# Latent attention: the doubled keys' scores of two maximum tiles formed together on both 64-row tiles of the array

## The chip, the cores and the metric

The kernel runs on one core of one Trainium2 chip. A core has a matrix engine (TensorE, PE in the profile, its weight loads PEld), VectorE (DVE), ScalarE (ACT), GpSimd (POOL) and SyncE (SP, which here only starts DMAs). Matmuls write to PSUM, which the program holds as one tile `PB` of eight banks of 512 columns. The metric is device time in microseconds, the median of several runs; lower is better. Beside the runs there is one profiled execution, from which all views below are taken.

## What is computed

Two layers of a backbone: windowed attention, then latent attention; the change is in the second layer. Cut to what matters:

```python
def attend(qn, qr, kn, kr, v):                 # 16 heads, 1024 queries, 256 + 1024 = 1280 keys
    s = (jnp.einsum("bqhd,bkhd->bhqk", qn, kn)     # 64 dimensions, keys of the head
         + jnp.einsum("bqhd,bkd->bhqk", qr, kr)) * scale   # 32 dimensions, keys shared by the heads
    p = jax.nn.softmax(s, axis=-1)
    return jnp.einsum("bhqk,bkhd->bqhd", p, v)
```

The softmax needs, for each query, a number to subtract before the exponential. The kernel takes the maximum over all 1280 keys of scores that are formed once in a cheap way (one matmul pass over the high parts), and then forms the scores proper, with the shift already added by one more row of the product.

## The kernel before

**Units.** The work of the layer's attention is cut into 32 units (class `UnitB`): a unit is one head and one half of the queries (512). Unit number `ui` belongs to head `ui // 2`; `e` is the head's place in its pair, `half` the half of the queries. The order of PE, ACT and DVE is the order of the code (a manual schedule), POOL and SP follow the recorded order too. What decides when something runs is therefore the place in the loop over `units` and the semaphores between engines.

**The array in two row tiles.** The keys have 64 rows (64 dimensions), so two products of 64 rows run side by side on the upper and the lower half of the array: `t` = 0 and 1. The 1280 keys lie in `kt` and `kr1` as 768 columns on each half: columns 0 to 511 hold keys 0 to 511 on rows 0 to 63 and keys 512 to 1023 on rows 64 to 127; columns 512 to 767, the last 256 keys, stand on both halves. These are the doubled keys.

**Maximum tiles** (`top(b)`, b = 0 to 3, 128 queries each). Four matmuls of 512 columns (L1260, two passes on two row tiles) fill two banks; then the doubled keys' part, two matmuls of 256 columns (L1263), both on the row tile `b % 2`, fill half of a third bank. VectorE reduces the 1280 columns to a negated maximum (L1265). All four tiles use the same three banks `psm`, so each tile's first matmul waits for the reduction before it.

**Shift** (`shift`): PE transposes the four columns of maxima into `pm_bank` (L1269), VectorE spreads them (L1270), ScalarE copies (L1275).

**Scores** (`score(i, a, b)`, i = 0 to 4, 256 keys each): five passes on two row tiles, ten matmuls of 512 columns (L1291; the fifth pass, of 36 rows, adds the shift), into one of two pairs of banks (`slot()` alternates). `expo(i)` on ScalarE takes the exponential of the 1024 columns (L1297), after which GpSimd adds up the sums (L1301, L1305). A slot is free for the next score when its exponential is done.

**Values and the finish.** `PV` multiplies the exponentials by the values (20 matmuls, L1313) into `pv_bank`; `fin` copies half of it (L1328, ACT), `fin1` adds the other half (L1332, DVE); `fin2` transposes the sums (L1342), VectorE reduces them (L1343) and, for every second head, takes the reciprocal (L1346); `fin3` (L1357, L1358, L1360) scales the output.

**The order in one round of the loop** (unit `u`; `pu`, `ppu` are the units before it, `nu`, `nnu` after it): u.score(0) with nu.top(2) inside it after two of its five passes; u.score(1) with nu.top(3) inside it after four; products that make keys for the next pair in two rounds of four (`make_K`, L126 to L128); pu.PV; nu.shift; fin3 of ppu and fin2 of pu; nnu.top(0); pu.fin1; u.score(2), u.score(3), nnu.top(1), u.score(4). The rounds with `ui % 8 == 0` also make values (`make_V`), with fin1 ahead of that. So a round, from one PV to the next, holds 25 score pairs (a pair is the same pass on both row tiles), eight pairs of L1260 and eight single L1263.

Of the kernel before, what the change touches and what calls it, by code (L numbers as in the profile page):

```python
# [13 lines left out]
ALU = mybir.AluOpType  # L14
AX = mybir.AxisListType
# [6 lines left out]
TOK = SEQ + CTX  # L22
# [38 lines left out]
def kernel(ctx: ExitStack, tc: tile.TileContext, t, out, dbg=None):  # L61
    nc = tc.nc
# [4 lines left out]
    PB = ppool.tile([128, 8, 512], F32, name="PB")  # L67
# [56 lines left out]
    def mm3(o, a, b, first, last):  # L124
        (ah, al), (bh, bl) = a, b
        nc.tensor.matmul(o, ah, bh, start=first, stop=False)  # L126
        nc.tensor.matmul(o, al, bh, start=False, stop=False)  # L127
        nc.tensor.matmul(o, ah, bl, start=False, stop=last)  # L128
# [177 lines left out]
    class Pieces:  # L306
# [6 lines left out]
        def load(self, n=1):  # L313
            for _ in range(n):
                if self.todo:
                    bi, k = self.todo.pop(0)
                    c0 = blocks[bi]
                    st = shp(stg.next(), 2, 256)
                    src = w_in[k * 128 : (k + 2) * 128, c0 : c0 + 256]
                    load(out=st, in_=src.rearrange("(k p) n -> p k n", p=128))  # L320
                    self.held.append((bi, k, st))
# [119 lines left out]
    def proj_t(bi, gp, c):  # L441

        W = wt[bi]
        ps = pss()
        if gp:
            o = shp(ps, 2, 256)
            m = [hw[gp][:, :, s] for s in range(2)]
        else:
            o = ps[:, 0:258]
            m = [hT[0][:, s] for s in range(2)]  # L450
        cs = slice(c * 128, c * 128 + 128)
        for k in range(8):
            b = [x[:, :, k, :] if gp else x[:, k, :] for x in m]
            mm3(o, [W[:, s, k, cs] for s in range(2)], b, k == 0, k == 7)
        if gp == 0:
            bias[bi, c] = biases()
            nc.vector.tensor_copy(bias[bi, c], ps[:, 256:258])
        return ps
# [330 lines left out]
    for i, (gp, c) in enumerate([(1, 0), (1, 1), (2, 0), (2, 1)]):  # L789
        held.append((1, gp, c, proj_t(1, gp, c)))  # L790
        if i == 0:
            ps = pst()
# [16 lines left out]
    for c in range(2):  # L809
        ps = proj_t(1, 0, c)  # L810
# [6 lines left out]
    for bi in range(2, 8):  # L817
        for i, (gp, c) in enumerate([(0, 0), (0, 1), (1, 0), (1, 1), (2, 0), (2, 1)]):
            ps = proj_t(bi, gp, c)
# [7 lines left out]
    for bi in (8, 9):  # L827
        for c in range(2):
            ps = proj_t(bi, 0, c)
# [38 lines left out]
    for ui, u in enumerate(units):  # L868
# [11 lines left out]
        for ci in range(u.m):  # L880
# [10 lines left out]
            i = u.g * u.m + ci - 1  # L891
# [182 lines left out]
    def g_tile(bi, p, half=None, bank=None):  # L1074
        c0 = blocks1[bi][1]
        W = wt1[bi]
        if half != 1:
            gps[bi] = pss() if bank is None else bank
        ps = gps[bi]
        for j in (0, 1) if half is None else (half,):  # L1080
            for k in range(8):
                mm3(
                    ps[:, j * 256 : j * 256 + 256],
                    [W[:, s, k, j * 128 : j * 128 + 128] for s in range(2)],
                    [hT1[p][:, s, k, :] for s in range(2)],
                    k == 0, k == 7,
                )
        if half == 0:
            return
        gg = ev.next()  # L1090
        nc.scalar.activation(gg, ps, AF.Silu)
        ch = (c0 - 800) // 128
        load(out=g1_d[ch : ch + 2, :, (p - 1) * 256 : p * 256].rearrange("c p n -> p c n"), in_=shp(gg, 2, 256))

    nx = norm_x(src1(4), xr, junk)
    for ti in range(NT):
        n = ti + 3
# [45 lines left out]
    kr1, kr2 = r_at(12, 768), (r_at(112, 512), r_at(15, 256))  # L1143
# [6 lines left out]
    otr = Ring(F, [0, 4], 1024)  # L1150
    rbr = Ring(F, [8, 9], 256)
    mxr = Ring(F, [44, 44.5], 128)
    psm = PB[:, 0:3, :]
    pm_bank = PB[:, 2, 256:384]
    slots = [PB[:, 3:5, :], PB[:, 5:7, :]]
    pv_bank = PB[:, 7, :]

    def slot():
        slots.reverse()
# [22 lines left out]
                nc.gpsimd.tensor_copy(kr[p : p + 4], const[p : p + 4, 0:1].to_broadcast([4, n]))  # L1182

    def make_V(quad, x, x0=psm[:, 0:2]):
        for t0, ps in ((0, x0), (4, PB[:, 7:8]), (2, x)):
            nt = min(2, NP - t0)
            for j in range(2 * nt):
                ti = 2 * t0 + j
                o = ps[:, j // 2, (j % 2) * 256 : (j % 2) * 256 + 256]
                for k in range(2):  # L1190
                    mm3(
                        o,
                        [ckvT[:, s, k, ti * 128 : ti * 128 + 128] for s in range(2)],
                        [ukV[:, s, k, quad * 256 : quad * 256 + 256] for s in range(2)],
                        k == 0, k == 1,
                    )
            nc.scalar.copy(
                Vq[:, 2 * t0 : 2 * t0 + 2 * nt].rearrange("p t h d -> p (t h d)"),
                ps[:, 0:nt].rearrange("p a b -> p (a b)"),
            )  # L1200
            yield
# [26 lines left out]
    class UnitB:  # L1228
# [24 lines left out]
        def top(self, b):  # L1253
            n, r1, _ = self.q
            bs = slice(b * 128, b * 128 + 128)
            pairs = ((n[:, 0, bs], self.kt[:, 0]), (r1[:, bs], kr1))
            rs = [slice(64 * t, 64 * t + 64) for t in range(2)]
            for i, (q, k) in enumerate(pairs):
                for t in range(2):
                    nc.tensor.matmul(psm[:, t], q[rs[t]], k[rs[t], 0:512], start=i == 0, stop=i == 1)  # L1260
            for i, (q, k) in enumerate(pairs):
                r = rs[b % 2]
                nc.tensor.matmul(psm[:, 2, 0:256], q[r], k[r, 512:768], start=i == 0, stop=i == 1)  # L1263
            flat = psm.rearrange("p a b -> p (a b)")[:, 0:TOK]
            nc.vector.reduce_max(self.mx[:, 32 + b : 33 + b], flat, AX.X, negate=True)  # L1265

        def shift(self):
            pm, r2 = pm_bank, self.q[2]
# [99 lines left out]
    yr = Ring(F, [10, 14, 18], 1024)  # L1368
    junk1 = f_at(44, 256).bitcast(BF16)
    ogr1 = Ring(R, [134, 142], 2048)  # L1370
    pso1 = Banks(0, 1, 2)

    def wo_pieces():
        st = f_at(45, 512)
# [115 lines left out]
    with tc.manual_schedule(engines={E.PE, E.Activation, E.DVE}):  # L1490
        kr = make_kr()
        ones_kr()
        next(kr)
        next(kr)
        g_tile(8, 3, 0, PB[:, 7, :])
        next(kr)
        g_tile(8, 3, 1)
        make_K(0, (0, 1), slot())
        g_tile(9, 3, 0, PB[:, 0, :])
        make_K(0, (2,), slot())  # L1500
        g_tile(9, 3, 1)
        next(vk)
        u0.top(0)
        next(vk)
        g_tile(8, 4, 0, slots[0][:, 0])
        u0.top(1)
        next(vk)
        u0.top(2)
        g_tile(8, 4, 1)
        units[2].prep()  # L1510
        u0.top(3)
        g_tile(9, 4, 0, slots[0][:, 1])
        u0.shift()
        u1.top(0)
        make_K(1, (0, 2), slots[1])
        u1.top(1)
        g_tile(9, 4, 1)
        nc.scalar.activation(warm, const[:, 1:2], AF.Exp)
        u1.top(2)
        for ui, u in enumerate(units):  # L1520
            pu, ppu = [units[ui - n] if ui >= n else None for n in (1, 2)]
            nu, nnu = [units[ui + n] if ui + n < NU else None for n in (1, 2)]
            if nnu and ui:
                nnu.prep()
            if ui == 0:
                u.score(0)
                nu.top(3)
                u.score(1)
                nu.shift()
                nnu.top(0)  # L1530
                u.score(2)
                u.score(3)
                nnu.top(1)
                u.score(4)
                continue
            u.score(0, 0, 2)
            if nu:
                nu.top(2)
            u.score(0, 2, 5)
            u.score(1, 0, 4)  # L1540
            if nu:
                nu.top(3)
            u.score(1, 4, 5, hold=True)
            x = slot()
            if ui % 4 == 0 and u.pair < 7:
                make_K(u.pair + 1, (0, 2), x)
            if ui % 4 == 1 and u.pair < 7:
                make_K(u.pair + 1, (1,), x)
            if ui == NU - 2:
                next(out_fill)  # L1550
            pu.PV()
            u.expo(1)
            if ui % 4 > 1 and ui < 23 or ui > 25:
                next(wo_fill)
            if ui == NU - 1:
                next(out_fill)
            pu.fin()
            if nu:
                nu.shift()
            if ppu and ppu.e == 1:  # L1560
                ppu.fin3(x[:, 0])
            pu.fin2(x[:, 1])
            if ui % 8 == 0:
                pu.fin1()
                for _ in make_V(u.pair // 2, x):
                    pass
            if nnu:
                nnu.top(0)
            if ui % 8:
                pu.fin1()  # L1570
            u.score(2)
            u.score(3)
            if nnu:
                nnu.top(1)
            u.score(4)
        u, pu = units[-1], units[-2]
        pu.fin3(slot()[:, 0])
        next(out_fill)
        next(out_fill)
        u.PV()  # L1580
        u.fin()
        u.fin1()
        next(out_fill)
        next(out_fill)
        u.fin2(slot()[:, 0])
        next(out_fill)
        next(out_fill)
        u.fin3(slot()[:, 0])
# [75 lines left out]
```

## Time and profile before

| what | before |
|---|---|
| median of 3 runs | 1629.61 us (1625.56 to 1631.41) |
| profiled execution, its own time | 1627.81 us |
| its span, first to last instruction | 1626.0 us |
| granted TensorE clock | 0.996 |
| attention rounds, first to 30th PV (1040.78 to 1503.01) | 462.2 us in 29 rounds |
| one plain round (1246.69 to 1260.83) | 14.14 us |
| a round with a `make_K` before its end (1260.83 to 1277.30) | 16.47 us |
| DVE, ACT and POOL busy in the plain round | 9.29, 6.95 and 11.78 us |

The page gives busy shares of the whole span; three quarters of it lies in other stages (the first layer, projections, the output product), which the change leaves alone. The lead-in of the attention, with the first seven maximum tiles and unit 0, is 998 to 1040.78 us; the rounds follow; after 1503.01 come the last unit and the output. The prediction shows the lines of the page, of the waits and of the timeline of one round.

### The profile page before, as it was taken

The numbers are of one execution on the slowest core, as the hardware profiler recorded it, in microseconds if no ns is written. First come the engines' busy times: TensorE is split into PE (matmuls) and PEld (weight loads), VectorE is DVE, ScalarE is ACT, GpSimd is POOL, SyncE is SP. The second block draws the span as 40 slices with busy tenths as digits, with TensorE's granted clock in tenths as the row PEclk, the third lists the DMA queues.
The fourth block names the chain that finished last, engine by engine and source line by source line (L and its number), as shares of the span: only waits on it lengthen the run. The fifth ranks groups of instructions, "written<-read, shape, count | busy, mean of one in ns | idle before, by whom it ended". The sixth has DMA issues, their size and how long they took to land.

```text
span 1626.0 us, 27118 instructions
## 1 busy us (share of the span) xinstructions
PE 1583.7 (97%) x9938; PEld 1239.6 (76%) x9938; DVE 926.6 (57%) x1993; ACT 804.4 (49%) x1558; POOL 700.7 (43%) x684
## 2 busy tenths in 40 slices
PE   7899999999999999998999999999999999999998
PEld 4787787887878888878998899666766766766587
DVE  3515461538888888878525203666566566566354
ACT  3432232359777777777413322554455455445321
POOL 1231121114453333344105240578688688688510
PEclk9999999999999999999999999999999999999999
DMA  6446775444333333326105753213233223244151
GB/s 248 162 146 207 223 202 169 122 148 115 98 107 95 92 92 92 91 97 215 42 14 147 263 155 98 71 46 92 59 95 94 73 78 89 65 127 116 55 173 65
DMA packets 147205, 192.70 MB, mean 119 GB/s; under 512 B 13936, under 2 KB 84208, under 8 KB 147072
## 3 DMA queue, kind: packets, MB, share of 16 engines
q1 hardware_dynamic: 145456, 188.94, 38.5%
q10 hardware_dynamic: 1616, 2.04, 0.4%
q8 instruction: 78, 1.28, 0.3%
q14 instruction: 55, 0.45, 0.1%
HBM read 144.77 MB, written 46.15 MB: 117 GB/s over the span
## 4 chain that ended last, share of the span: by engine, by line
PE 83%; ACT 5%; DVE 4%; issue 2%; DMA 1%; POOL 1%; POOLq 0%; DVEq 0%; SPq 0%; ACTq 0%
PE PB L126 14%; PE PB L127 14%; PE PB L128 14%; PE PB L1291 12%; PE PB L1313 8%; PE PB L1260 5%; PE PB L621 4%; PE PB L611 3%; PE PB L583 2%; PE PB L584 2%; ACT arena_f L593 1%; PE PB L181 1%; PE PB L1263 1%; ACT arena_r L121 1%; PE PB L1342 1%
## 5 line engine op out<-in xcount | busy, mean ns | idle before, releaser
L126 PE MATMUL PB<-arena_r 128*128 128x512 f32 (+3 forms) x1496 | 509.4, 342 | 4.5 <-ACT arena_r L387 1.6
L127 PE MATMUL PB<-arena_r 128*128 128x512 f32 (+3 forms) x1496 | 502.6, 336 | 3.3 <-DVE arena_r L388 1.6
L128 PE MATMUL PB<-arena_r 128*128 128x512 f32 (+3 forms) x1496 | 500.4, 335 | 0.0
L1305 POOL TENSOR_TENSOR arena_f<-arena_f 128x512 f32<-128x512 f32 x252 | 328.5, 1304 | 103.0 <-ACT arena_f L1297 86.7
L126 PEld LDWEIGHTS PB<-arena_r 128*128 128x128 f32 x1496 | 283.8, 190 | 49.7 <-issue 14.6
L127 PEld LDWEIGHTS PB<-arena_r 128*128 128x128 f32 x1496 | 284.8, 190 | 31.7 <-DVE arena_r L388 3.3
L128 PEld LDWEIGHTS PB<-arena_r 128*128 128x128 f32 x1496 | 284.6, 190 | 27.9
L1265 DVE TENSOR_REDUCE arena_f<-PB 128x1 f32<-128x1280 f32 x128 | 190.2, 1486 | 115.6 <-PE PB L1263 109.2
L122 POOL TENSOR_TENSOR arena_r<-arena_f,arena_r 128x512 fp32r<-128x512 f32 x88 | 115.0, 1322 | 308.0 <-ACT arena_r L121 252.4
L1291 PE MATMUL PB<-arena_r 64*128 64x512 f32 (+1 forms) x1600 | 229.1, 391 | 0.3 <-ACT arena_f L1297 0.3
L1297 ACT ACTIVATE arena_f<-PB 128x1024 f32<-128x1024 f32 x160 | 164.0, 1026 | 124.4 <-PE PB L1291 84.7
L1291 PEld LDWEIGHTS PB<-arena_r 64*128 64x128 f32 (+1 forms) x1600 | 175.2, 185 | 24.3 <-ACT arena_f L1297 1.8
L590 DVE CUSTOM_DVE_ANT_0 arena_f<-PB,arena_f,small 128x256 f32<-128x256 f32 (+1 forms) x288 | 145.0, 521 | 25.2 <-PE PB L584 18.6
L1313 PE MATMUL PB<-arena_f 128*64 128x512 f32 x640 | 144.4, 597 | 0.0
L122 DVE TENSOR_TENSOR arena_r<-PB,arena_r 128x512 fp32r<-128x512 f32 (+1 forms) x186 | 123.0, 670 | 22.3 <-ACT arena_r L121 21.5
L593 ACT ACTIVATE arena_f<-arena_f,small 128x640 f32<-128x640 f32 (+2 forms) x160 | 119.3, 746 | 28.4 <-DVE small L592 27.4
L621 PE MATMUL PB<-arena_r 128*128 128x512 f32 x336 | 123.7, 441 | 3.3 <-ACT arena_f L632 2.5
L121 ACT CAST arena_r<-arena_f 128x512 fp32r<-128x512 f32 (+2 forms) x137 | 82.3, 609 | 79.8 <-PE PB L128 12.1
L121 ACT CAST arena_r<-PB 128x512 fp32r<-128x512 f32 (+1 forms) x186 | 103.8, 569 | 31.9 <-PE PB L611 31.1
L611 PE MATMUL PB<-ident,arena_f 128*128 128x128 f32 x672 | 111.4, 274 | 1.4 <-ACT arena_f L593 0.9
L1313 PEld LDWEIGHTS PB<-arena_f 128*64 128x64 f32 x640 | 43.1, 136 | 81.4 <-issue 80.6
L1260 PE MATMUL PB<-arena_r 64*128 64x512 f32 x512 | 97.6, 433 | 1.8 <-DVE arena_f L1265 1.8
(180 smaller groups left out, 1985.6 us busy)
## 6 DMA issues: line engine op xcount, KB each, us to landing
arena_f<-ada_w SPq DMA_DIRECT2D x47, 512.0 KB, 5.6
arena_r<-q_d SPq DMA_DIRECT2D x80, 256.0 KB, 4.0
arena_r<-qn_d SPq DMA_DIRECT2D x64, 256.0 KB, 3.8
arena_r<-qr_d SPq DMA_DIRECT2D x192, 64.0 KB, 3.2
arena_f<-a_w_in SPq DMA_DIRECT2D x40, 256.0 KB, 3.2
arena_f<-x SPq DMA_DIRECT2D x16, 512.0 KB, 6.1
g_d<-arena_f SPq DMA_DIRECT2D x32, 256.0 KB, 2.3
q_d<-arena_f SPq DMA_DIRECT2D x64, 128.0 KB, 2.4
```

Source lines behind the costliest of these rows:

```text
L121: nc.scalar.copy(hi, src)
L122: (lo_eng or nc.vector).tensor_sub(lo, src, hi.bitcast(F32))
L126: nc.tensor.matmul(o, ah, bh, start=first, stop=False)
L127: nc.tensor.matmul(o, al, bh, start=False, stop=False)
L128: nc.tensor.matmul(o, ah, bl, start=False, stop=last)
L621: nc.tensor.matmul(self.pv, V[:, self.chunks[ci], self.g, :], PT[:, s], start=ci == 0 and s == 0, stop=ci == self.m - 1 and s == 1,)
L1260: nc.tensor.matmul(psm[:, t], q[rs[t]], k[rs[t], 0:512], start=i == 0, stop=i == 1)
L1265: nc.vector.reduce_max(self.mx[:, 32 + b : 33 + b], flat, AX.X, negate=True)
L1291: nc.tensor.matmul(S[:, t], k[r, c : c + 128], q[r], start=j == 0, stop=j == 4)
L1297: nc.scalar.activation(E, self.S, AF.Exp)
L1305: eng.tensor_add(self.acc, self.acc, E[:, t])
L1313: nc.tensor.matmul(self.pv[p : p + 64], Vq[:, cs[t], self.h % 4, :], E[:, t], start=i == 0, stop=i == 4)
```

## The change

A maximum tile no longer forms its doubled part itself. After tile 1 (and after tile 2) the doubled parts of tiles 0 and 1 (2 and 3) are formed by four matmuls of 256 columns (new L1269), one tile's on the upper row tile and the other's on the lower, into half a bank each of two banks that lie three apart (`rest`, banks 0 and 3). VectorE reduces a tile's first 1024 columns right after their four matmuls (new L1263), the two doubled parts together in one reduction with two results (new L1270), and after tile 3 takes the smaller of the two sets of negated maxima (new L1272). The banks are dealt anew: `psm` 1 to 3, of which the tiles now fill two, `pm_bank` in bank 3, `pv_bank` in bank 0, slots in 4 to 7. In the loop, u.score(1) is finished ahead of nu.top(3), and nnu.top(1) stands ahead of the last pass of u.score(3).

```diff
-    psm = PB[:, 0:3, :]
-    pm_bank = PB[:, 2, 256:384]
-    slots = [PB[:, 3:5, :], PB[:, 5:7, :]]
-    pv_bank = PB[:, 7, :]
+    psm = PB[:, 1:4, :]
+    pm_bank = PB[:, 3, 0:128]
+    slots = [PB[:, 4:6, :], PB[:, 6:8, :]]
+    pv_bank = PB[:, 0, :]
+    rest = PB[:, 0:4:3, 256:512]
...
-            for i, (q, k) in enumerate(pairs):
-                r = rs[b % 2]
-                nc.tensor.matmul(psm[:, 2, 0:256], q[r], k[r, 512:768], start=i == 0, stop=i == 1)
-            flat = psm.rearrange("p a b -> p (a b)")[:, 0:TOK]
-            nc.vector.reduce_max(self.mx[:, 32 + b : 33 + b], flat, AX.X, negate=True)
+            mx, flat = self.mx, psm[:, 0:2].rearrange("p a b -> p (a b)")
+            nc.vector.reduce_max(mx[:, 32 + b : 33 + b], flat, AX.X, negate=True)
+            if b in (1, 2):
+                b0 = b - b % 2
+                for i, (q, k) in enumerate(((n[:, 0], self.kt[:, 0]), (r1, kr1))):
+                    for t in range(2):
+                        c = slice((b0 + t) * 128, (b0 + t) * 128 + 128)
+                        nc.tensor.matmul(rest[:, t], q[rs[t], c], k[rs[t], 512:768], start=i == 0, stop=i == 1)
+                nc.vector.reduce_max(mx[:, 104 + b0 : 106 + b0], rest, AX.X, negate=True)
+            if b == 3:
+                nc.vector.tensor_tensor(mx[:, 32:36], mx[:, 32:36], mx[:, 104:108], ALU.min)
...
-            u.score(1, 0, 4)
+            u.score(1, hold=True)
             if nu:
                 nu.top(3)
-            u.score(1, 4, 5, hold=True)
...
             u.score(2)
-            u.score(3)
+            u.score(3, 0, 4)
             if nnu:
                 nnu.top(1)
+            u.score(3, 4, 5)
             u.score(4)
```

The lead-in, `make_V` and the output take their banks by the same new numbers (7 becomes 0; 0 to 2 become 1 to 3 in the output product).

**Place 1, PE, second half of a round.** Rows of before, from nnu.top(1) to nu.top(2) of the next round: L1260 and L1263 are the maximum tile, the L1291 after it score(4) (ten), then the first two passes of score(0) (four).

```order
L1260 MATMUL PB<-arena_r 128x512 [waits DVE_49]
L1260 MATMUL PB<-arena_r 128x512 x3
L1263 MATMUL PB<-arena_r 128x256 x2
L1291 MATMUL PB<-arena_r 128x512 [waits Activation_49]
L1291 MATMUL PB<-arena_r 128x512 x9
L1291 MATMUL PB<-arena_r 128x512 [waits Activation_49]
L1291 MATMUL PB<-arena_r 128x512 x3
L1260 MATMUL PB<-arena_r 128x512 [waits DVE_49]
```

The same place in the changed program; L1261 and L1269 are the maximum tile, L1298 the scores, of which the first two are the last pass of score(3).

```order
L1261 MATMUL PB<-arena_r 128x512 [waits DVE_49]
L1261 MATMUL PB<-arena_r 128x512 x3
L1269 MATMUL PB<-arena_r 128x256 [waits DVE_49]
L1269 MATMUL PB<-arena_r 128x256 x3
L1298 MATMUL PB<-arena_r 128x512 x2
L1298 MATMUL PB<-arena_r 128x512 [waits Activation_49]
L1298 MATMUL PB<-arena_r 128x512 x9
L1298 MATMUL PB<-arena_r 128x512 [waits Activation_49]
L1298 MATMUL PB<-arena_r 128x512 x3
L1261 MATMUL PB<-arena_r 128x512 [waits DVE_49]
```

Four doubled matmuls stand where two stood, with a wait for VectorE of their own, and the last pass of score(3) has moved behind the tile, so that between it and score(0), which takes the same slot, only score(4) is left. The wait values in the built program say which instruction each wait is for: the wait of L1269 is for the addition of fin1 (new L1339), which reads bank 0, and the last wait shown here, that of tile 2, is for the reduction of the doubled parts (new L1270), not for that of the tile's own two banks (new L1263): the view `rest` runs from bank 0 to bank 3, and the banks between it count as read. The wait of tile 3 is for L1270 in the same way.

**Place 2, DVE, the same stretch.** Before, from the reduction of fin2 to the maximum tiles of one unit: four reductions of 1280 columns with the addition of fin1 between the first and the second.

```order
L1343 TENSOR_REDUCE small<-PB 128x4 [waits PE_49]
L1265 TENSOR_REDUCE arena_f<-PB 128x1 [waits PE_49]
L1332 TENSOR_TENSOR arena_f<-PB,arena_f 64x512 [waits DMAHW4_49,Activation_49]
L1265 TENSOR_REDUCE arena_f<-PB 128x1 [waits PE_49] x3
L122 TENSOR_TENSOR arena_r<-arena_f,arena_r 128x512 [waits DMAHW7_49,DMAHW6_49,Activation_49]
```

In the changed program (L1350, L1339 are fin2 and fin1):

```order
L1350 TENSOR_REDUCE small<-PB 128x4 [waits PE_49]
L1263 TENSOR_REDUCE arena_f<-PB 128x1 [waits PE_49]
L1339 TENSOR_TENSOR arena_f<-PB,arena_f 64x512 [waits Activation_49]
L1263 TENSOR_REDUCE arena_f<-PB 128x1 [waits PE_49]
L1270 TENSOR_REDUCE arena_f<-PB 128x2 [waits PE_49]
L1263 TENSOR_REDUCE arena_f<-PB 128x1 [waits PE_49]
L1270 TENSOR_REDUCE arena_f<-PB 128x2 [waits PE_49]
L1263 TENSOR_REDUCE arena_f<-PB 128x1 [waits PE_49]
L1272 TENSOR_TENSOR arena_f<-arena_f 128x4 [waits DVE_49]
```

Two reductions with two results and a small minimum are added; the reductions of the doubled parts stand between those of tiles 1 and 2 and of tiles 2 and 3.

More of the change, by code (lines that the diff above doesn't have):

```diff
@@ L1184, in make_V @@
     def make_V(quad, x, x0=psm[:, 0:2]):
-        for t0, ps in ((0, x0), (4, PB[:, 7:8]), (2, x)):
+        for t0, ps in ((0, x0), (4, PB[:, 0:1]), (2, x)):
             nt = min(2, NP - t0)
@@ L1370 @@
     ogr1 = Ring(R, [134, 142], 2048)
-    pso1 = Banks(0, 1, 2)
+    pso1 = Banks(1, 2, 3)
     def wo_pieces():
@@ L1494 @@
         next(kr)
-        g_tile(8, 3, 0, PB[:, 7, :])
+        g_tile(8, 3, 0, pv_bank)
         next(kr)
@@ L1498 @@
         make_K(0, (0, 1), slot())
-        g_tile(9, 3, 0, PB[:, 0, :])
+        g_tile(9, 3, 0, psm[:, 0])
         make_K(0, (2,), slot())
@@ L1571 @@
             u.score(2)
-            u.score(3)
+            u.score(3, 0, 4)
             if nnu:
                 nnu.top(1)
+            u.score(3, 4, 5)
             u.score(4)
```

## The prediction

> **What bounds the kernel now.** I read the page first, for the engine that is the bound, and then the chain.
>
> ```profile
> PE 1583.7 (97%) x9938; PEld 1239.6 (76%) x9938; DVE 926.6 (57%) x1993; ACT 804.4 (49%) x1558; POOL 700.7 (43%) x684
> PE 83%; ACT 5%; DVE 4%; issue 2%; DMA 1%; POOL 1%; POOLq 0%; DVEq 0%; SPq 0%; ACTq 0%
> ```
>
> TensorE is the bound, and everything else hides under it. The windows view (length, then each engine's busy time) of the 29 rounds together and of one plain round:
>
> ```profile
> 1040.78:1503.01 462.23, 462.23 (x3216) 302.62 (x3215) 286.36 (x295) 233.37 (x304) 353.87 (x274) 1.00 0.30 82
> 1246.69:1260.83 14.14, 14.14 (x100) 8.67 (x99) 9.29 (x9) 6.95 (x8) 11.78 (x10) 1.00 0.31 83
> ```
>
> PE is busy in 100% of the rounds, so busy time shows no loss there: matmuls overlap, and the record of the last one covers a gap. Waits show on the weight loads instead. The view of the waits, for the 29 rounds (1040.78 to 1503.01), columns: microseconds in total, times, longest:
>
> ```profile
> PEld PB L1260 <- DVE arena_f L1265: 23.1, 58, 0.4
> ```
>
> 58 waits are two a round, 0.40 us each: the first matmul of a maximum tile waits for the 1280-column reduction of the tile before. To see which tiles, and what a step costs, I read the timeline of one plain round, from PV at 1246.69 to the next at 1260.83 (start, length, engine, line):
>
> ```profile
> 1251.82 0.73 PE L1260 MATMUL PB<-arena_r 64*128 64x512 f32 x4
> 1252.38 0.28 PE L1263 MATMUL PB<-arena_r 64*128 64x256 f32 x1
> 1252.38 0.39 PE L1291 MATMUL PB<-arena_r 64*128 64x512 f32 x1
> 1252.50 0.28 PE L1263 MATMUL PB<-arena_r 64*128 64x256 f32 x1
> 1252.62 2.25 PE L1291 MATMUL PB<-arena_r 64*128 64x512 f32 x18
> 1254.70 0.39 PE L1291 MATMUL PB<-arena_r 36*128 36x512 f32 x1
> 1254.94 0.40 PE L1260 MATMUL PB<-arena_r 64*128 64x512 f32 x2
> 1255.41 1.77 PE L1291 MATMUL PB<-arena_r 64*128 64x512 f32 x14
> 1257.17 0.72 PE L1260 MATMUL PB<-arena_r 64*128 64x512 f32 x4
> 1257.97 1.78 PE L1291 MATMUL PB<-arena_r 64*128 64x512 f32 x13
> 1259.71 0.73 PE L1260 MATMUL PB<-arena_r 64*128 64x512 f32 x4
> 1260.29 0.39 PE L1263 MATMUL PB<-arena_r 64*128 64x256 f32 x2
> 1260.52 0.39 PE L1291 MATMUL PB<-arena_r 36*128 36x512 f32 x1
> 1260.83 1.08 PE L1313 MATMUL PB<-arena_f 128*64 128x512 f32 x4
> ```
>
> Steps: 14 matmuls in 1.77 us are seven pairs, (1.77 - 0.39) / 6 = 0.23 (0.231 over several rows). The two L1263 take 1252.38 to 1252.62, 0.12 each. A tile that starts after a wait or a change of row tiles has its second pair 0.73 - 0.39 = 0.34 after the first: a cold start costs 0.105.
>
> The row to look at is the L1291 at 1252.38. In the program both L1263 stand ahead of it, yet it starts with the first of them, on the other row tile. **The doubled part does not hold both row tiles**: the free one runs ahead with the scores, and as tiles 0 and 1 load different row tiles, the two are even again at 1255.41. So only the parts of tiles 2 and 3 are lost, since a common wait (1259.71) and PV (1260.83) stop the tile that ran ahead. The Trainium skill, page "TensorE: Matmul & The Clock Gate", section "The mechanism", says that matmuls start and end strictly in program order; by that rule the four parts, 0.24 each, would hold both row tiles, and pairing alone would save 0.47 a round, some 14 us over 30. The rows at 1252.38 and 1252.50 contradict it, and I give it no weight.
>
> **The change part by part.**
>
> *Maximum tile and doubled part on PE.* Work per row tile stays the same (four times 0.12 a round); what can go is the lag at tiles 2 and 3 and the two waits. Without any wait the round would be: from 1252.38, 25 score pairs and six L1260 pairs, 31 x 0.231 = 7.16, doubled parts 0.47, the switch to PV 0.10 (0.33 instead of 0.23): PV at 1260.11, 0.72 earlier. That is the ceiling, and three waits stand against it.
>
> *New wait 1: fin1.* The first doubled part now writes bank 0, which fin1's addition reads.
>
> ```profile
> 1252.82 1.49 DVE L1265 TENSOR_REDUCE arena_f<-PB 128x1 f32<-128x1280 f32 x1
> 1254.34 0.68 DVE L1332 TENSOR_TENSOR arena_f<-PB,arena_f 64x512 f32<-64x512 f32 x1
> L1343 DVE TENSOR_REDUCE small<-PB 128x4 f32<-128x512 f32 x32 | 22.0, 689 | 0.5
> ```
>
> The reductions of 512 and 1280 columns (0.69, 1.49) give 1.044 ns a column, so an estimate of 1.22 us for 1024, 0.27 less. L1332 then starts at 1254.07, ends at 1254.75, and with 0.05 for the signal (below) releases PE at 1254.80. PE wants the doubled part after score(2), four passes of score(3) and the tile, 11 x 0.231: 1254.92. A wait costs nothing if it ends before 1254.92 - 0.105. So no cost here; behind it in PE's queue stands all the rest of the round. Where VectorE has the reciprocal ahead of the reduction, it is later:
>
> ```profile
> 1205.73 1.44 DVE L1265 TENSOR_REDUCE arena_f<-PB 128x1 f32<-128x1280 f32 x1
> 1207.20 0.69 DVE L1332 TENSOR_TENSOR arena_f<-PB,arena_f 64x512 f32<-64x512 f32 x1
> 1222.79 1.44 DVE L1265 TENSOR_REDUCE arena_f<-PB 128x1 f32<-128x1280 f32 x1
> 1224.26 0.69 DVE L1332 TENSOR_TENSOR arena_f<-PB,arena_f 64x512 f32<-64x512 f32 x1
> ```
>
> The same sum from these rows: seven rounds with the reciprocal (1205.73) lose 0.18, four with fin3 too (1222.79) lose 0.34. The three rounds with make_V have fin1 ahead of the tile and lose nothing; the other 15 have no margin to speak of (0 to 0.03), so the bound for this wait is 2.6 us (as summed) to 5.
>
> *New wait 2: score(0) for the exponential of score(3).* They share a slot. Before, tile 1 and score(4) stand between them, now score(4) alone. The last unit, which has no maximum tiles, shows that spacing, for scores 2 and 4:
>
> ```profile
> 1508.14 3.36 PE L1291 MATMUL PB<-arena_r 64*128 64x512 f32 x24
> 1509.69 1.02 ACT L1297 ACTIVATE arena_f<-PB 128x1024 f32<-128x1024 f32 x1 [0.55 <-PE PB L1291]
> 1510.77 0.53 PEld L1291 LDWEIGHTS PB<-arena_r 64*128 64x128 f32 x6 [0.47 <-ACT arena_f L1297]
> 1255.28 1.03 ACT L1297 ACTIVATE arena_f<-PB 128x1024 f32<-128x1024 f32 x1 [0.19 <-PE PB L1291]
> 1207.38 0.39 PE L1291 MATMUL PB<-arena_r 36*128 36x512 f32 x1
> 1206.75 2.18 ACT L1297 ACTIVATE arena_f<-PB 128x1024 f32<-128x1024 f32 x2 [0.19 <-PE PB L1291]
> ```
>
> The exponential ends at 1510.71 and PE goes on at 1510.77: 0.05 for the signal, and PE did wait there. For score(3) of the plain round, ScalarE starts at 1255.28, 0.58 after the last pass at 1254.70; in the round with the reciprocal at 1206.75 + 2.18 - 1.03 = 1207.90, 0.52 after it. In the new order: doubled part 1254.92 to 1255.16, last pass of score(3) at 1255.16, score(4), and score(0) wanted at 1256.55; released at 1255.16 + 0.58 + 1.03 + 0.05 = 1256.82. It starts 0.27 late and cold: 0.37 a round, 0.32 where ScalarE starts after 0.52. ScalarE is otherwise free then (6.95 of 14.14 us busy).
>
> *Old waits.* Tile 2 now waits for the doubled reduction of tiles 0 and 1. Tile 1's second pair at 1254.69 ends 0.39 later; then 0.04, 1.14 until the next reduction starts, 0.69 and 0.05: 1257.00, and PE comes at 1257.38 because of wait 2. Gone. Tile 3: tile 2's second pair at 1257.61, its reductions done at 1259.92; PE wants the tile after the doubled part and eight score pairs at 1259.93. It still starts cold, at 1259.92, second pair 1260.26, PV 1260.58. **Before 1260.83: 0.25 gained**, of a ceiling of 0.72.
>
> The price of the doubled reduction, two results from two banks, is in no row: one bank of 512 columns is 0.69, 1280 columns across three banks are 1.49; between these I take 0.69, since 1280 columns across banks show no price for the crossing. The minimum after tile 3 lies under PV, as make_K's and the splits' VectorE work does:
>
> ```profile
> L603 DVE TENSOR_TENSOR small<-small 128x4 f32<-128x4 f32 x40 | 11.8, 296 | 6.9 <-ACT small L599 6.9
> 1246.69 4.51 PE L1313 MATMUL PB<-arena_f 128*64 128x512 f32 x20
> ```
>
> It is 0.30 us beside 4.5; without that cover the transposes of the shift would wait for it. Order on SP, POOL and ACT is unchanged and the tiles issue no DMA. POOL, 11.8 us in a plain round, is under 13.9.
>
> *Sum,* by `ui % 4`: eight rounds of 1 (fin3, no reciprocal) 0.26 (2.1), seven of 2 (plain) 0.25 (1.75), seven of 3 (reciprocal; 0.32 at wait 2) 0.14 (1.0), four of 0 (both; 0.32, and tile 1 waited before too, to 1222.79 + 1.44 + 0.05) 0.06 (0.2), three of 0 with make_V 0.33 (1.0): 6.0 us. Lead-in, from its waits (998 to 1040.78):
>
> ```profile
> PEld PB L1260 <- DVE arena_f L1265: 3.2, 4, 1.6
> PEld PB L1263 <- DVE arena_r L1270: 1.1, 2, 0.5
> ```
>
> Three of seven doubled parts there have no scores beside them and go (0.7), the two waits of L1263 for the shift go (0.55 of delay), the first round gains 0.3, the longest wait grows by the doubled reduction less the shorter first one (-0.69 + 0.27), and the first shift has its maxima 0.2 sooner: 1.4, bounds 0 and 2. Together 7.4 us: **1627.8 - 7.4 = 1620.4 us**, against the profiled execution's 1627.81; the median shown is 1.8 above that. I own to a spread of 4 us, as each wait is a small difference of two long sums.
>
> **The rivals.** (Half a per cent, 8.1 us, is about what a measurement can tell from no change; the line is 1619.7.)
> - *One new wait is not there*: wait 2, about 0.34 x 30 = 10 more, 1610; or tile 3 in time, its cold start of 0.1 x 30 = 3 more, 1617. For: tile 3 misses by 0.1 only. Against: the last unit shows wait 2 as it is. Both gone: the ceiling, 0.72 x 29 + 1.4, 1605.
> - *The doubled parts don't run side by side*, as the change says they do: two loads every 0.12 us is a rate no row shows (two every 0.23, or one every 0.12). At worst 0.23 more a round, +7: 1627, no change.
> - *Slower: the doubled reduction is dear.* At price 0.69 + x, tile 3 comes x later, and above x = 0.27 tile 2 as well. The gain is gone at 0.94 us; from 1.1 us the kernel is over half a per cent slower; at 1.2 us 0.5 a round more than before: 1641. For: two banks that don't adjoin are in no row. Against: 1.044 ns a column across three banks.
>
> **Chances.** My sum 0.62 (own range 1616 to 1625, 0.26 of it below the line), one new wait absent 0.11, both 0.04, side by side fails 0.14, dear reduction 0.09. Faster 0.26 + 0.15 = 0.41, no change 0.36 + 0.14 = 0.50, slower 0.09. The range takes in all but the ceiling and the dear reduction: 1609 to 1631.
>
> **What would show it.** Right: the profile after has PE waiting for ScalarE's exponential once a round, about 0.35 us; waits of L1261 for VectorE once a round instead of twice, for L1270; waits of L1269 for fin1's addition in 11 rounds; a plain round of 13.9 us; L1263 at 1.22 and L1270 at 0.69 us; the second pair of L1269 0.12 after the first. Wrong: plain rounds of 13.5 (no new wait) or 14.1 and more; L1270 over 0.94 us; a wait of PV for L1270, which by the sum ends at 1259.87 while PV starts at 1260.58.

## The result, and the profile after

| what | before | after |
|---|---|---|
| median | 1626.62 us (1625.56 to 1631.41, 6 runs) | 1621.12 us (1618.86 to 1622.09, 6 runs) |
| ratio after / before | | 0.9953, 95% interval 0.9941 to 0.9966 |
| profiled execution, its own time | 1627.81 us | 1622.09 us |
| span | 1626.0 us | 1620.3 us |
| start to the attention's first maximum tile | 998.07 us | 998.93 us |
| lead-in, from there to the first PV | 42.71 us | 42.24 us |
| 29 rounds, first to 30th PV | 462.23 us | 456.22 us |
| the rest | 122.97 us | 122.92 us |

By the ratio of the runs the gain is 0.47%; the two medians lie 5.5 us (0.34%) apart. The interval leaves out 1, so there is a gain, but it is just under the half per cent that was put down as the bound of what can be told from no change: the likeliest case of the prediction, at 1620.4 us. In the profiled execution the span is 5.7 us shorter and the rounds alone 6.0; how the lead-in brought half a microsecond only is read below.

The page after, the engines' line, and the windows view (length, busy time of PE, PEld, DVE, ACT, POOL, then granted clock, DMA share and GB/s) of the 29 rounds and of one plain round:

```profile
PE 1574.6 (97%) x9938; PEld 1222.6 (75%) x9938; DVE 964.9 (60%) x2089; ACT 803.9 (50%) x1558; POOL 701.1 (43%) x684
1041.17:1497.39 456.22, 454.13 (x3217) 285.44 (x3216) 322.24 (x381) 232.94 (x304) 354.35 (x275) 1.00 0.30 83
1244.29:1258.21 13.92, 13.82 (x102) 8.28 (x100) 10.54 (x11) 6.95 (x8) 11.81 (x10) 1.00 0.33 86
```

PE has the same 9938 matmuls and is still the bound. In the plain round it now shows 0.10 us without work, where before it was busy in all 14.14: a new wait is long enough to outlast the overlap of the matmuls. The waits of the weight loads in the 29 rounds (microseconds in total, times, longest) name it:

```profile
PEld PB L1298 <- ACT arena_f L1304: 14.5, 29, 0.5
PEld PB L1261 <- DVE arena_f L1270: 7.5, 29, 0.3
PEld PB L1269 <- DVE arena_f L1339: 5.4, 19, 0.4
PEld PB L1261 <- DVE arena_f L1263: 0.8, 4, 0.2
```

Where 58 waits for the 1280-column reduction stood, there is one wait a round for an exponential, one for the reduction of the doubled parts, and some for fin1's addition. They are the two new waits that the prediction named, and the late tile 3. The plain round after, in the timelines of PE, of the weight loads and of VectorE (start, length, engine, line; idle time before and what ended it in brackets):

```profile
1249.99 2.25 PE L1298 MATMUL PB<-arena_r 64*128 64x512 f32 x18
1252.08 0.62 PE L1261 MATMUL PB<-arena_r 64*128 64x512 f32 x4
1252.53 0.40 PE L1269 MATMUL PB<-arena_r 64*128 64x256 f32 x4
1252.76 2.40 PE L1298 MATMUL PB<-arena_r 36*128 36x512 f32 x16
1254.41 0.30 PEld L1298 LDWEIGHTS PB<-arena_r 64*128 64x128 f32 x4 [0.53 <-ACT arena_f L1304]
1254.99 0.63 PE L1261 MATMUL PB<-arena_r 64*128 64x512 f32 x4
1255.46 0.40 PE L1269 MATMUL PB<-arena_r 64*128 64x256 f32 x4
1256.81 0.68 DVE L1270 TENSOR_REDUCE arena_f<-PB 128x2 f32<-128x512 f32 x1
1257.54 0.30 PEld L1261 LDWEIGHTS PB<-arena_r 64*128 64x128 f32 x4 [0.25 <-DVE arena_f L1270]
1257.56 0.72 PE L1261 MATMUL PB<-arena_r 64*128 64x512 f32 x4
1258.21 0.65 PE L1320 MATMUL PB<-arena_f 128*64 128x512 f32 x2
```

Four doubled matmuls take 1252.53 to 1252.76, 0.12 a pair: they do run side by side. Then score(3)'s last pass and score(4), and at 1254.41 score(0) starts only when the exponential has freed its slot. Tile 2 follows at 1254.99 with no wait. Tile 3 is released at 1256.81 + 0.68 + 0.05 = 1257.54, cold: four matmuls in 0.72 instead of 0.62. Counted from PV, the prediction's steps stand beside this round as follows (us):

| step in the plain round | predicted | measured |
|---|---|---|
| first doubled part | 8.23 | 8.24 |
| score(3), last pass | 8.47 | 8.47 |
| score(0), after its wait | 10.13 | 10.12 |
| tile 2 | 10.69 | 10.70 |
| tile 3 | 13.23 | 13.27 |
| next PV | 13.89 | 13.92 |

The new instructions on VectorE, in the groups (busy time, mean ns of one, idle time before):

```profile
L1263 DVE TENSOR_REDUCE arena_f<-PB 128x1 f32<-128x1024 f32 x128 | 156.1, 1219 | 103.1 <-PE PB L1261 102.6
L1270 DVE TENSOR_REDUCE arena_f<-PB 128x2 f32<-128x512 f32 x64 | 43.6, 681 | 0.0
L1272 DVE TENSOR_TENSOR arena_f<-arena_f 128x4 f32<-128x4 f32 x32 | 33.9, 1060 | 1.1
```

The two reductions cost what was taken (1.22 and 0.69). The minimum costs 1.06 us instead of 0.30.

### The profile page after: what moved, and what is told of

It is laid out like the page before. It is cut to its first block, busy times and chain, and to the rows that moved or that the text cites. A ratio compares the mean times of both kernels' runs of the same rounds, so it can differ in the third digit from the quotient of the medians.

```text
span 1620.3 us, 27188 instructions
## 1 busy us (share of the span) xinstructions
PE 1574.6 (97%) x9938; PEld 1222.6 (75%) x9938; DVE 964.9 (60%) x2089; ACT 803.9 (50%) x1558; POOL 701.1 (43%) x684
## 4 chain that ended last, share of the span: by engine, by line
PE 81%; ACT 6%; DVE 4%; issue 2%; POOL 1%; DMA 1%; ACTq 0%; POOLq 0%; SPq 0%; DVEq 0%
PE PB L126 14%; PE PB L127 14%; PE PB L128 14%; PE PB L1298 10%; PE PB L1320 8%; PE PB L1261 4%; PE PB L621 4%; PE PB L611 3%; PE PB L583 2%; ACT arena_f L1304 2%; PE PB L584 2%; PE PB L181 1%; ACT arena_f L593 1%; PE PB L1269 1%; PE PB L1349 1%
## 5 line engine op out<-in xcount | busy, mean ns | idle before, releaser
L1263 DVE TENSOR_REDUCE arena_f<-PB 128x1 f32<-128x1024 f32 x128 | 156.1, 1219 | 103.1 <-PE PB L1261 102.6
L1298 PE MATMUL PB<-arena_r 64*128 64x512 f32 (+1 forms) x1600 | 211.0, 397 | 2.4 <-ACT arena_f L1304 0.3
L1298 PEld LDWEIGHTS PB<-arena_r 64*128 64x128 f32 (+1 forms) x1600 | 145.6, 186 | 42.9 <-ACT arena_f L1304 16.7
L611 PEld LDWEIGHTS PB<-ident,arena_f 128*128 128x128 f32 x672 | 83.5, 140 | 20.4 <-ACT arena_f L593 5.1
```

What stands on the lines that cost most here:

```text
L611: nc.tensor.transpose(pt[:, h, :], self.Ps[h][:, ci * 128 : ci * 128 + 128], ident)
L1263: nc.vector.reduce_max(mx[:, 32 + b : 33 + b], flat, AX.X, negate=True)
L1298: nc.tensor.matmul(S[:, t], k[r, c : c + 128], q[r], start=j == 0, stop=j == 4)
```

## The experiments

Theory: in every plain round two things hold back what the pairing makes room for, the wait of score(0) for the exponential of score(3) (0.37 us with the cold start), and the dependence of tiles 2 and 3 on the reduction of the doubled parts, which is not one of data: the view `rest` runs from bank 0 to bank 3 and takes in the banks of the tile (0.10). Rivals: that the reductions are themselves too long for the round, so that a wait stays whatever the banks; that the pairing alone brings the gain, since the doubled parts hold both row tiles (matmuls in program order); that the respacing alone brings it. Edits are to the changed kernel, where nothing else is said. Each ratio is to runs of the kernel before that were made beside the experiment; their median was 1628.97 us for the first four experiments and 1629.75 for the last two, against 1626.62 in the table above, so kernels of different tables are compared by ratios and by the rounds of their profiles.

**own_banks.** The doubled parts get two adjoining banks, the tile two others.

```diff
-    psm = PB[:, 1:4, :]
-    pm_bank = PB[:, 3, 0:128]
+    psm = PB[:, 2:4, :]
+    pm_bank = PB[:, 1, 0:128]
-    rest = PB[:, 0:4:3, 256:512]
+    rest = PB[:, 0:2, 256:512]
```

> The changed kernel with the banks dealt so that the doubled parts lie in banks 0 and 1 and the tiles in 2 and 3; nothing else differs, but tiles 2 and 3 now wait for the reduction of their own two banks and no longer for that of the doubled parts. My theory (the view that runs across the tiles' banks makes tile 3 start cold): the cold start of tile 3 goes, 0.10 us a round, plain round 13.90 to 13.80, some 3 us in all, about 1618 us; the wait for ScalarE stays. Rival (tile 3 starts cold since VectorE is late with tile 2's own reduction): nothing moves, 13.90 and 1621.

Measured: 1618.32 us (1615.89 to 1620.41, 5 runs), ratio to before 0.9934 (0.9921 to 0.9946). A plain round in the windows view, then waits of the weight loads over the whole span, then tile 3 in that round:

```profile
1242.30:1256.09 13.79, 13.69 (x101) 8.34 (x100) 10.81 (x11) 6.95 (x8) 11.82 (x10) 1.00 0.32 85
PEld PB L1298 <- ACT arena_f L1304: 16.8, 34, 0.7
1254.79 0.68 DVE L1270 TENSOR_REDUCE arena_f<-PB 128x2 f32<-128x512 f32 x1
1255.53 0.63 PE L1261 MATMUL PB<-arena_r 64*128 64x512 f32 x4
```

Tile 3 takes 0.63 instead of 0.72 and no wait of L1261 for L1270 is left; the wait for the exponential is as it was. The round is 0.13 shorter than the one shown above (0.10 to 0.13 over the plain rounds), the 29 rounds 3.1 us: the dependence came from the span of the view and cost one cold start a round. The intervals of the two ratios overlap, so the verdict rests on the rounds of the profile more than on the totals.

**late_tile1.** Tile 1 goes behind the whole of score(3), so that tile and score(4) stand again between score(3) and score(0).

```diff
-            u.score(3, 0, 4)
+            u.score(3)
             if nnu:
                 nnu.top(1)
-            u.score(3, 4, 5)
             u.score(4)
```

> The changed kernel with tile 1 behind the whole of score(3) again, as before the change; score(1) stays whole ahead of tile 3. My theory: the wait of score(0) for ScalarE (0.37 a round) goes, since the tile stands between them again; tile 2 comes 0.23 after the release it had and waits for the doubled reduction instead, about 0.33; the wait for fin1 shrinks by 0.23. Plain round 13.87, the rounds with a reciprocal 0.2 shorter, about 3 us less than the changed kernel, 1618 us. Rival (the wait for ScalarE comes from ScalarE being busy, not from the spacing): it stays, and the time grows by the new wait, 1630.

Measured: 1619.79 us (1615.86 to 1621.91, 5 runs), ratio 0.9941 (0.9929 to 0.9954). A plain round, and the waits over the span:

```profile
1239.35:1253.22 13.87, 13.82 (x102) 8.31 (x100) 10.62 (x11) 6.95 (x8) 11.81 (x10) 1.00 0.35 88
PEld PB L1261 <- DVE arena_f L1270: 24.5, 61, 1.9
PEld PB L1298 <- ACT arena_f L1304: 2.2, 5, 0.7
```

The exponential's wait is gone from the rounds, and nearly all of its time is back at tile 2, which now comes before the reduction of the doubled parts has ended: 61 waits for L1270 instead of 31. One wait was covering the other. The rounds with the reciprocal gain more: 0.16 us on average, where fin1's wait goes as well, and 0.30 (15.83 to 15.53) where fin3 stands too and that wait shrinks; 4 of its 19 waits are left. The 29 rounds are 2.7 us shorter; the intervals of the ratios overlap, so the totals alone do not show it.

**own_late.** Both edits together.

> Both edits together: doubled parts in banks of their own and tile 1 behind the whole of score(3). My theory: no wait is left in a round but 0.11 for fin1 in four rounds; plain round near the ceiling of the prediction, 13.43 us, 29 rounds about 15 us shorter than in the changed kernel, about 1606 us. Rival (the two row tiles don't run four doubled matmuls in 0.24 us, or GpSimd with 11.8 us a round becomes the bound): plain round 13.6 to 13.8, 1612 or more.

Measured: 1606.18 us (1605.39 to 1607.54, 4 runs), ratio 0.9861 (0.9847 to 0.9874). The 29 rounds, a plain round, and the waits over the span:

```profile
1040.77:1482.76 441.99, 441.99 (x3216) 290.99 (x3215) 290.33 (x380) 233.12 (x304) 357.25 (x274) 1.00 0.31 86
1237.52:1251.00 13.48, 13.48 (x102) 8.48 (x100) 8.98 (x11) 6.96 (x8) 12.07 (x10) 1.00 0.33 87
PEld PB L1298 <- ACT arena_f L1304: 2.2, 5, 0.7
PEld PB L1261 <- DVE arena_f L1263: 1.6, 2, 1.3
PEld PB L1269 <- DVE arena_f L1339: 0.9, 4, 0.2
```

No wait of a score or of tiles 1 to 3 is left in the plain round, and the total is near the ceiling of 1605 that the prediction put to both waits gone. Alone the edits take 3.1 and 2.7 us off the rounds, together 14.2. This version beats both kernels, the changed one by 14.9 us of median (ratios to before 0.9861 and 0.9953). That the two waits were what the change left lying, and that they hid each other, is shown by the three runs.

**spacing_alone.** To the kernel before: only the two tiles moved, as the change moves them; each still forms its own doubled part.

```diff
-            u.score(1, 0, 4)
+            u.score(1, hold=True)
             if nu:
                 nu.top(3)
-            u.score(1, 4, 5, hold=True)
...
-            u.score(3)
+            u.score(3, 0, 4)
             if nnu:
                 nnu.top(1)
+            u.score(3, 4, 5)
             u.score(4)
```

> The kernel of before with the new order of the scores alone: score(1) whole ahead of tile 3, tile 1 ahead of the last pass of score(3); each tile forms its own doubled part and VectorE reads 1280 columns. My theory: the wait for ScalarE comes (0.3), the wait of tile 2 goes (0.28), and at tile 3 and PV the row tiles lose less: plain round 14.0 instead of 14.14, about 4 us less than before, 1622 to 1623 us; most of what the whole change gives. Rival (what is gained comes from forming the doubled parts together): no gain, 1627 or more.

Measured: 1629.16 us (1626.66 to 1630.79, 11 runs), ratio 0.9997 (0.9988 to 1.0006): nothing, where a gain of about 4 us was expected. Waits over the span:

```profile
PEld PB L1291 <- ACT arena_f L1297: 16.3, 33, 0.7
PEld PB L1260 <- DVE arena_f L1265: 9.0, 38, 1.6
```

The waits did change places as thought (before, the maximum tiles had all of them), and the plain round fell to 14.04 to 14.08 us (13.94 in the first), about as expected. The 29 rounds took 461.62 us, 0.6 less than before. The miss is that I had worked out the plain round and counted the others like it. On average the rounds with fin3 stayed (14.55 to 14.56 us) as did those with the reciprocal (16.13), and those with both rose (15.85 to 15.95): there tile 1, one pass earlier than before, meets the 1280-column reduction of tile 0 and shows the step of a cold start (0.33 us). The trace shows the same wait, smaller, in the rounds with fin3 and in those with the reciprocal: tile 1 starts 0.06 us after that reduction ends, and on one row tile its second pair comes 0.33 us after the first; in the plain rounds it starts 0.16 to 0.20 after the end, with 0.24 between the pairs. Tile 2 then comes about 0.1 us later than in the plain round, which is what the plain round gained; that this is the whole cause was not tested.

**pairing_alone.** The changed kernel with tiles 3 and 1 at their old places.

```diff
-            u.score(1, hold=True)
+            u.score(1, 0, 4)
             if nu:
                 nu.top(3)
+            u.score(1, 4, 5, hold=True)
...
-            u.score(3, 0, 4)
+            u.score(3)
             if nnu:
                 nnu.top(1)
-            u.score(3, 4, 5)
             u.score(4)
```

> The changed kernel with the order of the scores of before (tile 3 after four passes of score(1), tile 1 behind the whole of score(3)): the doubled parts formed together and read apart, in the old places. My theory: tiles 2 and 3 each come after seven score pairs, while the doubled reduction releases them 2.31 us after the tile's second pair; both wait 0.23 and start cold, 0.33 each. Plain round 14.1, as before the change; about 7 us more than late_tile1, 1626 to 1627 us, no change against before within half a per cent. Rival (matmuls keep program order, so forming the parts together saves 0.47 a round wherever it stands): plain round 13.7, 1615 us.

Measured: 1626.05 us (1624.86 to 1627.36, 11 runs), ratio 0.9977 (0.9968 to 0.9986). A plain round and the waits over the span:

```profile
1244.59:1258.72 14.13, 14.01 (x102) 8.39 (x100) 10.42 (x12) 6.95 (x8) 11.86 (x10) 1.00 0.32 83
PEld PB L1261 <- DVE arena_f L1270: 31.4, 61, 2.0
PEld PB L1298 <- ACT arena_f L1304: 2.2, 5, 0.7
```

With the old spacing the plain round is 14.13, as good as before: two waits a round for L1270 stand where two for L1265 stood. The 29 rounds took 460.43 us, 1.8 less than before, and the lead-in 41.29, 1.4 less: that is most of the 0.23%. So of the 6.0 us that the change takes off the rounds, spacing alone brings 0.6 and pairing alone 1.8; the rest needs both. The rival as it was put, that pairing saves 0.47 a round wherever it stands, falls: by it the round would have come to about 13.7. Whether matmuls keep program order this run cannot settle, since its two waits could have swallowed such a gain; the rows of before settle that.

**fin1_first.** The theory of the wait for fin1: with the addition ahead of the reduction of tile 0 on VectorE in every round, the doubled part should not wait for it, and tile 1 should wait instead.

```diff
+            pu.fin1()
             if ui % 8 == 0:
-                pu.fin1()
                 for _ in make_V(u.pair // 2, x):
                     pass
             if nnu:
                 nnu.top(0)
-            if ui % 8:
-                pu.fin1()
             u.score(2)
```

> The changed kernel with the addition of fin1 ahead of tile 0 in every round, as the rounds with new values have it, so that VectorE does it before the reduction of tile 0. My theory (PE waits for whichever of the two comes second): the waits of the doubled part for fin1 go in all rounds, but tile 0's reduction ends 0.6 later and tile 1 waits for it, 0.35 to 0.5 a round; plain round 14.25, the whole about 10 us slower than the changed kernel, 1631. Rival (only the doubled part waits for VectorE there, tile 1 has room): the 2.6 us that wait 1 was put at are gained, 1618.

Measured: 1634.36 us (1633.91 to 1637.39, 7 runs), ratio 1.003 (1.002 to 1.004). A plain round, then the waits of the weight loads over the span:

```profile
1248.75:1263.09 14.34, 14.07 (x102) 8.24 (x100) 9.65 (x11) 6.95 (x8) 11.79 (x10) 1.00 0.32 83
PEld PB L1261 <- DVE arena_f L1263: 20.4, 26, 1.1
PEld PB L1298 <- ACT arena_f L1304: 16.8, 34, 0.7
```

No wait of L1269 for fin1's addition is left, and tile 1 waits for the reduction of tile 0 in all 26 rounds without `make_V`: it starts 0.55 us behind the score pair ahead of it in the plain round, where 0.23 is a step, and 1.08 behind it in the rounds with the reciprocal and fin3. The direction is that of the theory. The plain round came out at 14.33 to 14.36 us (14.25 in the first), 0.1 over what was put down. The 29 rounds took 469.85 us, 13.6 more than in the changed kernel, where about 10 were put down; most of the difference lies in the rounds with the reciprocal (0.6 us longer each), whose tile 1 is held longer than I had worked out. So the place of fin1's addition in the change, behind the first reduction, is worth more than the wait it causes.

## Why the prediction came out

*The doubled parts do not hold both row tiles.* Right, and shown by the rows of before: the score at 1252.38 starts with the first L1263, ahead of the second at 1252.50, and in all 29 rounds a score starts with the first L1263 of tile 0. pairing_alone agrees, since pairing without spacing leaves the plain round where it was, but its waits for L1270 would hide a gain too. The rule of the Trainium skill (page "TensorE: Matmul & The Clock Gate", section "The mechanism"), that matmuls start strictly in program order, does not hold for the two row tiles in these rows. Had it been followed, the prediction would have been some 14 us of gain for the pairing, and the run gave 0.23% of about 1630 us, 3.7 (2.3 to 5.2 by its interval).

*Wait 2,* score(0) for the exponential. Right in size: released at 10.13 us by the sum and at 10.12 by the trace, 0.26 late and 0.10 cold in the plain round, and there in each of the 29 rounds.

*Wait 1,* the doubled part for fin1's addition. Right in place: only the seven rounds with the reciprocal and the four with fin3 too show a longer distance than 0.23 from the tile's last pair to the doubled part, 0.28 to 0.30 in the seven and 0.38 in the four. With the cold pair behind it (0.11) that is 0.17 and 0.26 us, where 0.18 and 0.34 were put. The profile counts 19 waits, since short idle times of the weight loads count as well.

*Tile 3.* Right: released at 13.27 against 13.23, cold. That it hung on the view's span and not on the data was in the sum, and own_banks shows it.

*The rounds.* 6.0 us by the sum, 462.23 - 456.22 = 6.01 measured. That the two agree so closely is partly luck: the classes below are off by up to 0.04 a round, and the errors cancel. By class, predicted and measured: fin3 0.26 and 0.25, plain 0.25 and 0.29, reciprocal 0.14 and 0.12, both 0.06 and 0.02, with `make_V` 0.33 and 0.37.

*The lead-in.* 1.4 us by the sum, 0.5 in the profiled execution. The cause is not one of the waits of the sum: the granted clock fell there. The windows view of the last two maximum tiles ahead of the lead-in's second shift, of the changed kernel and then of late_tile1, whose lead-in has the same code:

```profile
1024.60:1030.68 6.08, 5.32 (x33) 4.03 (x33) 3.62 (x4) 2.20 (x4) 1.27 (x1) 0.72 0.79 217
1022.03:1026.93 4.90, 3.99 (x32) 2.69 (x32) 3.21 (x4) 1.79 (x4) 1.28 (x1) 1.00 0.80 210
```

The same stretch took 6.08 us at a mean clock of 0.72 and 4.90 at 1.00, 1.18 more. At the end of the last reduction 0.76 of it had built up. The other 0.41 is the minimum that follows it, again in the changed kernel and in late_tile1:

```profile
1030.05 0.57 DVE L1272 TENSOR_TENSOR arena_f<-arena_f 128x4 f32<-128x4 f32 x1
1026.72 0.16 DVE L1272 TENSOR_TENSOR arena_f<-arena_f 128x4 f32<-128x4 f32 x1
```

In the first a GpSimd addition was running, in the second it had just ended. In late_tile1, fin1_first and pairing_alone the whole lead-in took 41.07, 41.09 and 41.29 us, 1.4 to 1.6 less than the 42.71 of before: the term was right to 0.2, and the one execution disturbed. Why the clock fell after an idle time of PE that was no longer than in the other executions (1.74 to 1.75 us in each) stays open.

*The remaining 0.9 us.* In the profiled execution the stages ahead of the attention, which the change leaves alone but for bank numbers, ended 0.86 us later than before. Over the eight profiled executions of this study that point lies between 996.35 and 1001.69 us, so single spans of these kernels are compared to no better than a few microseconds, and rounds far better. That 1621.12 lies so near the forecast time of 1620.4 is luck in part as well: the median of before was 1629.61 us in three runs and 1626.62 in six, and the medians fell by 5.5 us where 7.4 was forecast.

*The minimum.* Mis-sized, 0.30 for 1.06 us, at no cost seen in the rounds, since it lies under PV, as the prediction had it.

*The rivals.* Side by side held (0.12 a pair), the doubled reduction was not dear (0.68), and no new wait was absent. What I hadn't foreseen is that removing one wait alone would have brought so little: the prediction gave 10 us for wait 2 absent, and late_tile1, which moves it away by order, brought 2.7 in the rounds, because the wait for the doubled reduction stood right behind it.

## What to carry to other kernels

A wait that ends last covers the next one: before a step is moved to cure a stall, work out what the following instructions wait for at their new times, since here two cures took 3.1 and 2.7 us off the rounds each, and 14.2 together. In this program, a reader of a buffer that is cut out of several banks by a stride is waited for by what writes the banks between them; where partners can adjoin, they should. And a new order is checked in each kind of round, not in the plainest alone: spacing_alone gained 0.1 us there and nothing in total.

## What the hardware showed that was not expected

The small minimum, 4 columns from SBUF to SBUF on VectorE, took 1.06 us on average. In the rounds it ended each time about when the GpSimd addition ended that was running as it started. The timelines of VectorE and GpSimd in the changed kernel, for the plain round and for the first such minimum, with GpSimd idle:

```profile
1245.67 1.12 DVE L1272 TENSOR_TENSOR arena_f<-arena_f 128x4 f32<-128x4 f32 x1
1244.14 2.62 POOL L1312 TENSOR_TENSOR arena_f<-arena_f 128x512 f32<-128x512 f32 x2
1014.05 0.16 DVE L1272 TENSOR_TENSOR arena_f<-arena_f 128x4 f32<-128x4 f32 x1
```

It ended at 1246.79, GpSimd's second addition at 1246.76; with nothing on GpSimd it took 0.16 us. The Trainium skill, page "SBUF — State Buffer", section "Who interferes with whom", states that VectorE and GpSimd share a pair of ports under an exclusive lock, and that a VectorE instruction with two SBUF inputs contends with a GpSimd instruction that reads SBUF. The trace agrees, with 1.12 against 0.16 us. An operation counted at 0.3 us by a row of another stage can so cost as much as the GpSimd instruction beside it, and the shift would have waited for it, had PV not lain over it. In the lead-in, which has no PV, the second shift did wait; in late_tile1, where that minimum took 0.16 instead of 0.57 us, the same wait was 0.8:

```profile
PEld PB L1276 <- DVE arena_f L1272: 1.2, 1, 1.2
```
